# One step of a hybrid recurrent decoder: TensorE's order fixed by hand in the chain and the LRU stage, LRU begun among x's last projections, sample runs joined, products moved ahead of transpositions, projections reordered

## The chip, the core and the metric

The kernel runs on one core of one Trainium2 chip. The core's engines are TensorE (PE, matrix products; PEld is its weight load), VectorE (DVE), ScalarE (ACT), GpSimd (POOL) and SyncE (SP), which only issues transfers here. They run side by side and wait for one another by semaphores. The metric is the time of one execution in device microseconds (us). TensorE has a clock that is granted in steps; the profile gives it as a share of full speed.

## What is computed

One layer for 512 prompt tokens and 8 x 8 sample tokens (N = 576 columns), width 1024, all in float32. Cut to what matters:

```python
u, za, xb, zb, q, zc, gates = split_in(rmsnorm(x) @ w_in)
oa = rwkv7_branch(u, za, ...)      # per head: s = s*w + sa (kk*a) + v k,  o = s r
ob = rglru_branch(xb, zb, ...)     # conv, two gates, h = a*h + sqrt(1-a^2)*gate*xc
oc = cross_attn(q, zc, mem_k, mem_v)   # prompt: 256 memory rows; samples: own caches
g_a, g_b, g_c = split(sigmoid(gates), 3)
merged = g_a*(oa @ w_br_a) + g_b*(ob @ w_br_b) + g_c*(oc @ w_br_c)
y = rmsnorm(x + merged @ w_out)
```

## The kernel before

**Projections.** Every product with a weight matrix is cut into units of 128 output rows. A unit loads 512 KB of weights (`wraw`), ScalarE rounds them (`whi`, L280), VectorE subtracts (`wlo`, L281), and TensorE makes 48 products of 128\*128 with 288 columns: the high part with both halves of x, the low part with the high half (L355). Units wait in a list (`Stream`, L305 on); `st.go(n)` issues n steps of the unit in work, six products each, and `st.until(label)` issues until a unit is done. So the code of each stage says how many projections stand between its own small products. The weights of the next unit are fetched while the present one is in work. Units that a stage needs come first; the rest (`spill_units`: gates g, LRU input xb and gate zb, attention gate zc) fill in.

**What sets the order.** Each engine executes its instructions in one fixed order. A scheduler makes that order when the program is built, from the written order and its own costs. TensorE's too: a product written behind 37 units of projections can be put later or earlier than that.

**Stages.** Attention (L660 to L800) comes first: memory keys and values are projected (kv), the samples' caches come from DRAM in 512 KB tiles (`kn`), their keys are transposed (`skt`), scores sS and values sO are products of 32-column tiles. Then RWKV in four groups of two head pairs. For each group: `prep_a`, `prep_b`; `prep_c` (transpositions vt and bkt, then products m that give M, L990 to L996); `invert` (L1001): the diagonal blocks of M go to DRAM (d, L1006) and come back as X (L1011), VectorE solves 30 substitution steps in place (Xt and X, L1016 and L1018), copies the transpose XT, and xz and M's blocks return over DRAM (L1026 to L1032). Meanwhile `direct` makes R and Zt and `bonus` the bonus products, then 37 steps of projections. `invert2` needs xz: z (L1041) and w (L1050). `solved` makes U and W. Then the chain runs over eight chunks (`chain`, L1122 on): A from the state and ZR, UV plus A on VectorE, dS from UV and BKn, the state's sum, and the outputs (A again, L1113). Three runs for the samples (`sample_a`, `_b`, `_c`) stand behind chunks 1 to 6.

**LRU** (`lru_phase`): for eight blocks j a convolution, two gate products pg (L516), gates on ScalarE, a root over four blocks, and a scan (`scan`, L535 on): be = args \* gx on POOL (L543, L544), the scan he on VectorE (L546), its output times z, and a split into the operand oh, ol of branch b. All this runs beside the products of branches c and a (br2, br0); branch b (br1) needs the LRU's output. POOL adds branch a's products to `merged` (L452). Last comes the product with w_out (fo, L1349).

Of the kernel before, what the change touches and what calls it, by code (L numbers as in the profile page):

```python
# [9 lines left out]
F32 = mybir.dt.float32  # L10
# [8 lines left out]
P = 128  # L19
D = 1024  # L20
KC = 8
# [25 lines left out]
class Kern:  # L47
    def __init__(self, ctx, tc, ins, outs):
# [7 lines left out]
        self.dq = 0  # L56

# [4 lines left out]
    def transpose(self, out, in_, rows):  # L62

        self.nc.tensor.transpose(out, in_, self.ident[:rows, :rows])  # L64
# [151 lines left out]
    def softplus(self):  # L216
# [9 lines left out]
        nc.vector.tensor_scalar(self.c4, self.c4, -4.0, None, op0=ALU.mult)  # L226

# [77 lines left out]
class Stream:  # L305
# [24 lines left out]
    def step(self):  # L330
# [22 lines left out]
        for q, (a, b) in enumerate(((hi, xh), (hi, xl), (lo, xh))):  # L353
            for o, t0, m in parts:
                nc.tensor.matmul(self.ps[:, o:o + m], a[:, k, :], b[:, k, t0:t0 + m],  # L355
                                 start=(k == 0 and q == 0), stop=(k == KC - 1 and q == 2))
# [35 lines left out]
def spill_units(K, pool):  # L392
# [38 lines left out]
    us = [Unit(w, C_G + D * b + P * j, x, gate(K.gd[b, j]), f"g{b}{j}") for b in (2, 0, 1) for j in range(KC)]  # L431
    us += [Unit(w, C_ZC + P * j, x, silu2(K.ocz[j], K.ocd[j]), f"zc{j}") for j in range(KC)]
    us += [Unit(w, C_XB + P * j, x, conv_in(j), f"xb{j}") for j in range(KC)]
    us += [Unit(w, C_ZB + P * j, x, silu2(K.zbd[j]), f"zb{j}") for j in range(KC)]
    return us


def branch_units(K, pool, b, w, oh, ol, place, out=None):
# [3 lines left out]
    def mk(j):  # L442
        def use(pb):
# [7 lines left out]
            if place == "mid":  # L451
                nc.gpsimd.tensor_add(m, m, t)  # L452
# [7 lines left out]
def load_split(K, pool, src, oh, ol):  # L460
    nc = K.nc
    for k in range(KC):
# [5 lines left out]
def lru_phase(K, o2, then):  # L468
# [4 lines left out]
    with tc.tile_pool(name="lruc", bufs=1, reuse_waits="tile") as lc, tc.tile_pool(name="lru", bufs=2, reuse_waits="tile") as lp:  # L473
# [9 lines left out]
        ohl = []  # L483
# [21 lines left out]
        def gates(j):  # L505
            if j % 4 == 0:
                quad[j // 4] = lp.tile([P, 4, N], F32, tag="args", name="args")
# [3 lines left out]
            for q, bh in enumerate((K.bah, K.bxh)):  # L511
                g = lp.tile([P, N], F32, tag=f"g{q}", name=f"g{q}")
                for s in range(2):
                    pg = K.psb(f"pg{q}")[:, 0:HN]
                    cs = slice(HN * s, HN * s + HN)
                    nc.tensor.matmul(pg, wbd[q][:, j, :], xc[:, cs], start=True, stop=True)  # L516
# [3 lines left out]
            c4 = K.c4[:, j:j + 1]  # L520
            nc.vector.tensor_scalar(gr, gr, c4, c4, op0=ALU.mult, op1=ALU.add)
# [3 lines left out]
            nc.scalar.activation(ap_, gr[:, 0:TP], AF.Exp)  # L525
            nc.scalar.activation(as_[:, :, 1:9], smp(gr), AF.Exp)
            th = lp.tile([P, AE], F32, tag="th", name="th")[:, 0:N]
            nc.scalar.activation(th, gr, AF.Tanh, scale=-1.0)
            nc.scalar.activation(gr, gr, AF.Exp, scale=2.0)
            nc.vector.scalar_tensor_tensor(ar, gr, 1.0, th, op0=ALU.add, op1=ALU.mult)  # L530
            gx = lp.tile([P, N], F32, tag="gx", name="gx", bufs=4)
# [3 lines left out]
        def scan(j):  # L535
# [7 lines left out]
            nc.gpsimd.tensor_mul(bp_, ar[:, 0:TP], gx[:, 0:TP])  # L543
            nc.gpsimd.tensor_mul(bs_[:, :, 1:9], smp(ar), smp(gx))  # L544
# [5 lines left out]
            o = lp.tile([P, N], F32, tag="g0", name="lo")  # L550
            nc.vector.scalar_tensor_tensor(o[:, 0:TP], hp_, 0.5, z2[:, 0:TP], op0=ALU.mult, op1=ALU.mult)
            nc.vector.scalar_tensor_tensor(smp(o), hs_[:, :, 1:9], 0.5, smp(z2), op0=ALU.mult, op1=ALU.mult)
            split(nc, ohl[0][:, j, :], ohl[1][:, j, :], o)
# [4 lines left out]

        for j in range(4):
            conv(j)  # L560
            st.go(9 if j else 13)
            gates(j)
            if j == 3:
                then()
            st.go(3)
        st.until("br27")
        ohl = [o2.tile([P, KC, N], F32R, tag=tag, name=tag) for tag in ("oh", "ol")]
        roots(0)
        for j in range(4, KC):
            conv(j)  # L570
            st.go(4)
            scan(j - 4)
            st.go(3)
            gates(j)
            st.go(3)
        roots(4)
        for j in range(4, KC):
            scan(j)
            st.go(9)
# [7 lines left out]
    return ohl  # L587
# [72 lines left out]
def attention(K, xp, qs, qf, kv):  # L660


    nc, i, st = K.nc, K.i, K.st
# [3 lines left out]
    def p_scores(h, n):  # L667
# [3 lines left out]
        for tt in range(4):  # L671
            ps = K.psb(f"s{h}{tt}")
            for dc in range(2):
                for q, (a, b) in enumerate(((qh, kh), (qh, kl), (ql, kh))):
                    nc.tensor.matmul(ps[:, :NM], a[:, dc, tt * P:(tt + 1) * P], b[:, 2 * h + dc, :],
# [832 lines left out]
```

## Time and profile before

| | us |
|---|---|
| median of three runs | 1183.21 (1181.63 to 1183.48) |
| the profiled execution | 1184.47 |
| its span | 1182.7 |
| TensorE busy | 1145.4 (97%) |
| VectorE busy | 713.2 (60%) |
| ScalarE busy | 517.3 (44%) |
| POOL busy | 184.3 (16%) |
| attention, first kv product to first u product | 144.7 |
| first group, first U product to the end of its chain | 55.8 |
| last gate products of LRU to the product with w_out | 87.0 |

How to read it: the span is the profiled execution's first to last instruction; the profiled execution's time lies 1.26 us above the median. Busy shares are means over stages with different limits. A row of the timeline gives start, duration, engine, line, operation, the tile written and those read, the form (128\*64 is a product that uses 64 of the array's columns), the count, and in brackets the engine's idle time ahead with what ended it. A product of 288 columns is recorded once or twice, so a "x2" can be two products.

### The profile page before, as it was taken

Reading aid. Unit: us, or ns where it says so; the run is one execution under the profiler, and the core shown is the slowest. Engines: PE = TensorE matmul, PEld = TensorE weight load, DVE = VectorE, ACT = ScalarE, POOL = GpSimd, SP = SyncE. Lnnn points to the kernel's source line nnn. Section 1 sums busy time; section 2 is a strip of 40 time slices with the busy share of each in tenths; the row PEclk is TensorE's granted clock in tenths of the full one; section 3 lists DMA queues with packets and bytes.
Section 4 is the critical chain, followed back from the end, with each engine's and each line's share of the span. In section 5 each row is a group of like instructions: output and inputs, shape, how many; then the busy total and the mean of one; then the engine's idle time right before and its main releaser. Section 6 shows DMA issues by size and latency. Waiting matters only on the chain.

```text
span 1182.7 us, 25731 instructions
## 1 busy us (share of the span) xinstructions
PE 1145.4 (97%) x10567; PEld 1068.8 (90%) x10567; DVE 713.2 (60%) x1436; ACT 517.3 (44%) x1004; POOL 184.3 (16%) x311
## 2 busy tenths in 40 slices
PE   6999999999999999999999999999999999979997
PEld 4998877899998898988989989999889999979997
DVE  5345655238764687835788457874455386975633
ACT  5444544337324374243752336532444266442333
POOL 3010001010003210022100130101211012570031
PEclk9999999999999999999999999999999999998999
DMA  4447685522452233532233522345337665348412
GB/s 140 130 145 233 211 254 189 162 81 66 107 140 73 65 93 82 142 89 70 78 92 120 145 73 65 106 125 149 85 90 232 203 195 170 104 115 261 117 45 81
DMA packets 220623, 151.50 MB, mean 128 GB/s; under 512 B 52640, under 2 KB 196106, under 8 KB 220506
## 3 DMA queue, kind: packets, MB, share of 16 engines
q1 hardware_dynamic: 217242, 146.87, 42.1%
q10 hardware_dynamic: 3264, 2.99, 0.9%
q8 instruction: 83, 1.36, 0.5%
q14 instruction: 34, 0.28, 0.1%
HBM read 120.82 MB, written 29.01 MB: 127 GB/s over the span
## 4 chain that ended last, share of the span: by engine, by line
PE 79%; DVE 7%; ACT 5%; issue 3%; DMA 3%; POOL 2%; SPq 0%; DVEq 0%; ACTq 0%; POOLq 0%
PE u L355 13%; PE g L355 12%; PE br L355 9%; PE xb L355 4%; PE zc L355 4%; PE za L355 4%; PE fo L1349 4%; PE q L355 4%; PE zb L355 3%; PE kv L355 2%; PE m L990 1%; PE dS L1137 1%; DVE wlo L281 1%; DMA wraw<-in_w_mem_kv 1%; PE skt L64 1%
## 5 line engine op out<-in xcount | busy, mean ns | idle before, releaser
L280 ACT CAST whi<-wraw 128x1024 fp32r<-128x1024 f32 x129 | 135.4, 1050 | 292.6 <-PE g L355 90.7
L281 DVE TENSOR_TENSOR wlo<-wraw,whi 128x1024 fp32r<-128x1024 f32 x128 | 158.9, 1241 | 127.5 <-ACT whi L280 126.7
L355 PE MATMUL u<-xh,whi 128*128 128x288 f32 x400 | 92.2, 305 | 0.0
L355 PE MATMUL br<-oh,wlo 128*128 128x288 f32 x384 | 84.4, 302 | 4.4 <-DVE wlo L281 4.3
L355 PE MATMUL u<-xl,whi 128*128 128x288 f32 x400 | 88.6, 300 | 0.0
L355 PE MATMUL u<-xh,wlo 128*128 128x288 f32 x400 | 88.6, 299 | 0.0
L355 PE MATMUL br<-oh,whi 128*128 128x288 f32 x384 | 85.4, 305 | 3.0 <-ACT oh L592 2.9
L355 PE MATMUL g<-xh,whi 128*128 128x288 f32 x384 | 86.6, 304 | 0.0
L355 PE MATMUL g<-xh,wlo 128*128 128x288 f32 x384 | 84.7, 300 | 0.0
L355 PE MATMUL g<-xl,whi 128*128 128x288 f32 x384 | 84.4, 301 | 0.0
L355 PE MATMUL br<-ol,whi 128*128 128x288 f32 x384 | 84.2, 301 | 0.0
L355 PEld LDWEIGHTS u<-xh,whi 128*128 128x128 f32 x400 | 65.1, 188 | 5.5 <-issue 4.1
L355 PEld LDWEIGHTS br<-oh,wlo 128*128 128x128 f32 x384 | 63.5, 194 | 5.6 <-DVE wlo L281 5.6
L355 PEld LDWEIGHTS br<-oh,whi 128*128 128x128 f32 x384 | 63.7, 193 | 4.3 <-ACT oh L592 3.4
L355 PEld LDWEIGHTS u<-xl,whi 128*128 128x128 f32 x400 | 64.7, 188 | 2.0 <-issue 1.4
L355 PEld LDWEIGHTS u<-xh,wlo 128*128 128x128 f32 x400 | 64.7, 188 | 0.9 <-issue 0.2
L355 PEld LDWEIGHTS g<-xh,whi 128*128 128x128 f32 x384 | 62.3, 190 | 3.2 <-issue 3.1
L355 PEld LDWEIGHTS g<-xh,wlo 128*128 128x128 f32 x384 | 62.7, 190 | 1.2 <-issue 1.2
L355 PEld LDWEIGHTS br<-ol,whi 128*128 128x128 f32 x384 | 63.4, 193 | 0.1
L355 PEld LDWEIGHTS g<-xl,whi 128*128 128x128 f32 x384 | 62.4, 190 | 1.1 <-issue 1.1
L1016 DVE TENSOR_TENSOR Xt<-X 72x30 f32<-72x30 f32 (+14 forms) x120 | 39.3, 328 | 11.4 <-DMA X<-d 7.8
L1349 PE MATMUL fo<-wol,oh 128*128 128x256 f32 (+1 forms) x160 | 45.0, 282 | 0.0
(386 smaller groups left out, 2894.3 us busy)
## 6 DMA issues: line engine op xcount, KB each, us to landing
wraw<-in_w_in SPq DMA_DIRECT2D x89, 512.0 KB
wraw<-in_w_mem_kv SPq DMA_DIRECT2D x16, 512.0 KB
kn<-in_cache_mem_k SPq DMA_DIRECT2D x16, 512.0 KB
kn<-in_cache_mem_v SPq DMA_DIRECT2D x16, 512.0 KB
gd<-flt SPq DMA_DIRECT2D x24, 288.0 KB
gtt<-gd SPq DMA_DIRECT2D x24, 288.0 KB
wraw<-in_w_br_c SPq DMA_DIRECT2D x8, 512.0 KB
wraw<-in_w_br_a SPq DMA_DIRECT2D x8, 512.0 KB
```

The source lines that it names most:

```text
L64: self.nc.tensor.transpose(out, in_, self.ident[:rows, :rows])
L280: nc.scalar.copy(hi, raw)
L281: eng.tensor_sub(lo, raw, hi.bitcast(F32))
L355: nc.tensor.matmul(self.ps[:, o:o + m], a[:, k, :], b[:, k, t0:t0 + m], start=(k == 0 and q == 0), stop=(k == KC - 1 and q == 2))
L990: nc.tensor.matmul(pms[h][64 * w:64 * w + 64, P * (c - c0):P * (c - c0) + P], BK[64 * h:64 * h + 64, c, w, :], ZR[64 * h:64 * h + 64, c].r ...
L1016: nc.vector.tensor_mul(tv, X[:, 0:s, s:s + 1].to_broadcast([NQ, s, m]), X[:, s:s + 1, s + 1:].to_broadcast([NQ, s, m]))
L1137: nc.tensor.matmul(pS[hs, C * o.q:C * o.q + C], o.BKn[:, c, hs], o.UV[:, c, hs], start=True, stop=True, tile_position=(0, 64 * h))
L1349: nc.tensor.matmul(pos[t][:r, :W], a[:, k, t * P:t * P + r], b[:, k, :], start=(k == 0 and q == 0), stop=(k == KC - 1 and q == 2))
```

## The change

It does these things:

- `K.mm` and `K.transpose` pin a product into the written order while `K.pin` is set. It is set from `invert2` to the end of each group's chain, and in all of `lru_phase`. There the order on TensorE, projections included, is as written.
- `products` (m and M) comes ahead of `prep_c`'s transpositions, and the writes of d follow each pair's M; X's read is issued ahead of the transpositions. The filler ahead of `invert2` is 34 steps instead of 37, and `invert2` does both halves of z before both of w.
- The chain's filler is given per step (2 and 4 steps; 1 and 3 in the last group), and the sample runs stand next to chain products of the same form (`full`, `tiled`).
- Attention: keys are transposed from the q stage on, and sample scores and values stand in longer runs; loads of values are issued ahead.
- x's projections: zb, sixteen of g, xb, four of g, zc, four of g (before: g, zc, xb, zb).
- LRU begins after zc7 with four units of g left; branch units are added when x's are done. be and the sum into `merged` move from POOL to VectorE; the factor c4 goes into ScalarE's scale and bias. The splits of the LRU's first four outputs stand behind br27 (branch c's end), and the writes of the LRU's state rows behind br11.

```diff
+        if self.pin:
+            self.tc.keep_in_program_order(ins)
...
-    us = [... g ...]; us += [zc]; us += [xb]; us += [zb]
+    return zb + g[:16] + xb + g[16:-4] + zc + g[-4:]
...
-                nc.gpsimd.tensor_add(m, m, t)
+                nc.vector.tensor_add(m, m, t)
...
-            nc.gpsimd.tensor_mul(bp_, ar[:, 0:TP], gx[:, 0:TP])
-            nc.gpsimd.tensor_mul(bs_[:, :, 1:9], smp(ar), smp(gx))
+            nc.vector.tensor_mul(bp_, ar[:, 0:TP], gx[:, 0:TP])
+            nc.vector.tensor_mul(bs_[:, :, 1:9], smp(ar), smp(gx))
...
             for o in prs:
                 prep_b(o)
                 st.go(3)
+                scaled(o)
+                products(o)
+                st.go(3)
+            X = invert()
             for o in prs:
                 prep_c(o)
-                st.go(6)
-            invert(prs)
+                st.go(3)
+            substitute(prs, X)
             direct(prs)
             for o in prs:
                 bonus(o)
-            st.go(37)
+            st.go(34)
+            K.pin = True
             invert2(prs)
             solved(prs)
...
+            fulls = {1: lambda: sample_a(o0), 4: lambda: sample_c(o0), 5: lambda: sample_a(o1)}
+            tileds = {2: lambda: sample_b(o0), 3: lambda: [sample_o(o0), sample_in(o1)],
+                      6: lambda: sample_b(o1), 7: lambda: sample_o(o1)}
             for c in range(8):
-                chain(prs, c)
-                if c in (1, 4): ... sample_a, sample_b, sample_c
+                chain(prs, c, (2, 4) if g + 1 < NG else (1, 3), fulls.get(c, none), tileds.get(c, none))
+            K.pin = False
...
+        K.pin = True
+        conv(0)
+        st.go(8)
+        conv(1)
+        st.go(6)
+        gates(0)
+        ...
+        for j in (4, 5, 6):
+            conv(j + 1)
+            st.go(4)
+            then(range(3 * j - 12, min(3 * j - 9, KC)))
+            st.go(3)
+            gates(j)
+        st.until("br27")
+        ohl = operand(o2)
+        ...
+        gates(7)
+        roots(4)
         for j in range(4, KC):
+            st.go(5)
             scan(j)
-            st.go(9)
+            split(nc, ohl[0][:, j, :], ohl[1][:, j, :], keep[j][1])
+        K.pin = False
```

**z on TensorE, second group.** Before (g and u are projections, z the first product behind the inversion, of one pair at a time; 300 projections stand between the last m product and this z):

```order
L355 MATMUL g_6133<-xl,whi 128x288 x2
L355 MATMUL g_6133<-xh,wlo 128x288 x2
L355 MATMUL u_6210<-xh,whi 128x288 x2
L1041 MATMUL z_5925<-xz,M_5235 32x32 x9
L355 MATMUL u_6210<-xl,whi 128x288 x2
L355 MATMUL u_6210<-xh,wlo 128x288 x2
L355 MATMUL u_6210<-xh,whi 128x288 x2
L355 MATMUL u_6210<-xl,whi 128x288 x2
L355 MATMUL u_6210<-xh,wlo 128x288 x2
```

Now (every product of `K.mm` has that helper's line, L71; the two pairs take turns from the first z on, 214 projections behind the last m):

```order
L71 MATMUL g_6061<-xh,whi 128x288 x2
L71 MATMUL g_6061<-xl,whi 128x288 x2
L71 MATMUL g_6061<-xh,wlo 128x288 x2
L71 MATMUL z_6092<-xz,M_5348 32x32
L71 MATMUL z_6093<-xz,M_5492 32x32
L71 MATMUL z_6092<-xz,M_5348 32x32
L71 MATMUL z_6093<-xz,M_5492 32x32
L71 MATMUL z_6092<-xz,M_5348 32x32
L71 MATMUL z_6093<-xz,M_5492 32x32
```

z of both pairs moved to one place, with nothing between the first pair's z and the second's.

**A chain step on TensorE, first group, with the samples' transposition s0t.** Before:

```order
L1128 MATMUL A<-sbd_2475,ZR 128x128 x2
L355 MATMUL u_4497<-xl,whi 128x288 x2
L355 MATMUL u_4497<-xh,wlo 128x288 x2
L1137 MATMUL dS<-UV,BKn 64x64 x2
L355 MATMUL u_4598<-xh,whi 128x288
L1137 MATMUL dS<-UV,BKn 64x64 x2
L1113 MATMUL A<-UV,M_3281 64x64
L1113 MATMUL A<-UV,M_3428 64x64
L1113 MATMUL A<-UV,M_3281 64x64
L1113 MATMUL A<-UV,M_3428 64x64
L355 MATMUL u_4598<-xh,whi 128x288
```

Now:

```order
L65 MATMUL s0t<-ident,sn 128x128 x4
L71 MATMUL g_4369<-xh,whi 128x288 x2
L71 MATMUL g_4369<-xl,whi 128x288 x2
L71 MATMUL g_4369<-xh,wlo 128x288 x2
L71 MATMUL g_4369<-xh,whi 128x288 x2
L71 MATMUL g_4369<-xl,whi 128x288 x2
L71 MATMUL g_4369<-xh,wlo 128x288 x2
L71 MATMUL dS<-UV,BKn 64x64 x4
L71 MATMUL A<-UV,M_3393 64x64
L71 MATMUL A<-UV,M_3538 64x64
L71 MATMUL A<-UV,M_3393 64x64
L71 MATMUL A<-UV,M_3538 64x64
```

dS of both pairs stands in one piece and A behind it; the projections that stood inside moved ahead of dS and behind A. Counted over the whole program, neighbouring products change between whole-array and tiled form 332 times before and 210 times now.

**A scan of LRU on VectorE.** Before (he is the scan, gtt a branch's gate product, wlo the next unit's weights):

```order
L530 SCALAR_TENSOR_TENSOR args<-g_12440,th 128x576
L281 TENSOR_TENSOR wlo<-wraw,whi 128x1024
L546 SCALAR_TENSOR_TENSOR he<-ae,be 128x584 x2
L551 SCALAR_TENSOR_TENSOR lo<-he,z_12488 128x512
L552 SCALAR_TENSOR_TENSOR lo<-he,z_12488 128x64
L450 SCALAR_TENSOR_TENSOR gtt<-gtt,br_12503 128x576
L281 TENSOR_TENSOR wlo<-wraw,whi 128x1024
L593 TENSOR_TENSOR ol<-lo,oh 128x576
L551 SCALAR_TENSOR_TENSOR lo<-he,z_12575 128x512
L552 SCALAR_TENSOR_TENSOR lo<-he,z_12575 128x64
```

Now (be and the sum into merged stand here too):

```order
L294 TENSOR_TENSOR wlo<-wraw,whi 128x1024
L466 TENSOR_TENSOR merged<-merged,gtt 128x576
L557 TENSOR_TENSOR be<-args,gx 128x512
L558 TENSOR_TENSOR be<-args,gx 128x8x8
L557 TENSOR_TENSOR be<-args,gx 128x512
L560 SCALAR_TENSOR_TENSOR he<-ae,be 128x584
L558 TENSOR_TENSOR be<-args,gx 128x8x8
L564 SCALAR_TENSOR_TENSOR gx<-he,z_12318 128x512
L565 SCALAR_TENSOR_TENSOR gx<-he,z_12318 128x64
L560 SCALAR_TENSOR_TENSOR he<-ae,be 128x584
L464 SCALAR_TENSOR_TENSOR gtt<-gtt,br_12305 128x576
```

The product be, which POOL made, moved in front of the scan on VectorE, and the sum into merged in front of that. On TensorE 312 projections stand between the last gate products and branch b's first product, before 162.

More of the change, by code (lines that the diff above doesn't have):

```diff
@@ L62, in transpose, with mm @@
     def transpose(self, out, in_, rows):
-        self.nc.tensor.transpose(out, in_, self.ident[:rows, :rows])
+        ins = self.nc.tensor.transpose(out, in_, self.ident[:rows, :rows])
+        if self.pin:
+            self.tc.keep_in_program_order(ins)
+    def mm(self, *a, **kw):
+        ins = self.nc.tensor.matmul(*a, **kw)
+        if self.pin:
+            self.tc.keep_in_program_order(ins)
+        return ins
     def psb(self, name):
@@ L226, in softplus @@
         nc.vector.tensor_scalar(self.c4, self.c4, -4.0, None, op0=ALU.mult)
+        self.c4n, self.c8 = (self.cst.tile([P, 8], F32, name=n) for n in ("c4n", "c8"))
+        nc.vector.tensor_scalar(self.c4n, self.c4, -1.0, None, op0=ALU.mult)
+        nc.vector.tensor_scalar(self.c8, self.c4, 2.0, None, op0=ALU.mult)
     def norm_load(self, tp, src, rows):
@@ L465, in load_split, with lru_phase @@
         split(nc, oh[:, k, :], ol[:, k, :], t)
-def lru_phase(K, o2, then):
+def lru_phase(K, o2, merge, operand):
     nc, tc, i, pv = K.nc, K.tc, K.i, K.pv
@@ L557, in roots, with lru_out @@
             nc.scalar.activation(q4, q4, AF.Sqrt, scale=0.25)
-        for j in range(4):
[L560 to L570, printed above, removed]
+        K.pin = True
[4 more added lines that the diff above has]
+        gates(0)
+        conv(2)
+        st.go(5)
+        gates(1)
+        st.until("g17")
+        oa, then = merge()
+        conv(3)
+        st.go(4)
+        gates(2)
+        st.go(5)
+        gates(3)
+        st.go(5)
+        roots(0)
+        for j in range(4):
+            scan(j)
+            if j == 1:
+                conv(4)
+            st.go(5)
+        for j in (4, 5, 6):
+            conv(j + 1)
             st.go(4)
-            scan(j - 4)
+            then(range(3 * j - 12, min(3 * j - 9, KC)))
             st.go(3)
             gates(j)
+        st.until("br27")
+        ohl = operand(o2)
+        for j in range(4):
+            split(nc, ohl[0][:, j, :], ohl[1][:, j, :], keep[j][1])
             st.go(3)
+        gates(7)
         roots(4)
         for j in range(4, KC):
+            st.go(5)
             scan(j)
-            st.go(9)
+            split(nc, ohl[0][:, j, :], ohl[1][:, j, :], keep[j][1])
+        K.pin = False
+    return ohl, lambda: lru_out(K, lo_st, cv_st)
+def lru_out(K, lo_st, cv_st):
     lf = lo_st.rearrange("p a b -> p (a b)")
@@ L1035, in invert2, with half @@
         def invert2(prs):
-            for g0 in (0, 9):
+            def half(g0):
                 pzs = [K.psb("z1") for o in prs]
@@ L1054, in invert2 @@
                     nc.scalar.copy(o.M1[a:a + 32, g0:g0 + 9, b:b + 32], pw[a:a + 32, 0:288].rearrange("p (a b) -> p a b", b=32))
+            half(0)
+            half(9)
+            st.go(1)
+            above(0)
+            above(9)
+            st.go(3)
         def direct(prs):
@@ L1121, in plus_state, with chain @@
                 nc.vector.tensor_add(u, pA[o.br:o.br + 64, P * o.q:P * o.q + P], u)
-        def chain(os, c):
+        def chain(os, c, steps, full, tiled):
             cur, nxt = sbd[(c + 1) % 2], sbd[c % 2]
@@ L1148, in chain @@
                 o.cur = nxt[:, o.q, :]
-            st.go(4)
+            tiled()
+            st.go(steps[1])
         def state_out(o):
```

339 lines of the change are left out of this document (184 added, 155 removed).

## Prediction

> **What bounds the kernel now.** I read the page's totals first, then the chain of work that ended last, then single stretches of TensorE's timeline. The totals and the chain's shares:
>
> ```profile
> PE 1145.4 (97%) x10567; PEld 1068.8 (90%) x10567; DVE 713.2 (60%) x1436; ACT 517.3 (44%) x1004; POOL 184.3 (16%) x311
> PE 79%; DVE 7%; ACT 5%; issue 3%; DMA 3%; POOL 2%; SPq 0%; DVEq 0%; ACTq 0%; POOLq 0%
> ```
>
> TensorE is the bound, and the change neither adds nor removes a matmul (8807 in each program). So it can pay in two ways only: the same matmuls issue more densely, or TensorE waits less. Two prices come first. A stretch of the chain gives the pace of projections; a timeline of TensorE in the first group's chain gives the price of changing between whole-array matmuls (128\*128) and tiled ones:
>
> ```profile
> 466.62 36.80 PE g L355 x276
> ...
> 378.93 0.45 PE L1137 MATMUL dS<-UV,BKn 128*64 128x64 f32 x8
> 379.21 0.41 PE L1113 MATMUL A<-UV,M 128*64 128x64 f32 x8
> 379.55 0.53 PE L355 MATMUL u<-xh,whi 128*128 128x288 f32 x2
> ...
> 386.32 0.60 PE L64 MATMUL s0t<-ident,sn 128*128 128x128 f32 x4
> 386.75 0.61 PE L1128 MATMUL A<-sbd,ZR 128*128 128x128 f32 x4
> ...
> 387.82 0.34 PE L1137 MATMUL dS<-UV,BKn 128*64 128x64 f32 x4
> 388.09 0.40 PE L355 MATMUL u<-xh,whi 128*128 128x288 f32 x1
> 388.42 0.34 PE L1137 MATMUL dS<-UV,BKn 128*64 128x64 f32 x4
> 388.58 0.40 PE L1113 MATMUL A<-UV,M 128*64 128x64 f32 x8
> 388.92 0.40 PE L355 MATMUL u<-xh,whi 128*128 128x288 f32 x1
> ```
>
> A projection costs 36.80/276 = 0.133 us, a transposition (386.75 − 386.32)/4 = 0.11. One projection between two dS pairs takes 388.42 − 388.09 = 0.33 instead of 0.13, so each of its two changes costs 0.10. Compared whole, the step with that projection inside takes 388.92 − 387.82 = 1.10, less 0.13 for the projection 0.97; the step with both pairs together takes 379.55 − 378.93 = 0.62. That is 0.35 for two changes, 0.17 each, because the tiled matmuls also overlap better when more stand together.
>
> **Part 1, the order on TensorE.** Counted in the two orders, 332 changes of tile form become 210: 98 fewer in the four groups (inversion and chain), 24 fewer in attention. 122 at 0.10 is 12 us, at 0.17 it is 21. I take 19.5 (0.16 each), as most removed ones are of the dS kind. The Trainium skill ("TensorEngine Tiling (Array Packing)", Tiling Modes, Key Properties) says that a change of tiling mode drains TensorE and a change of tile alone does not. By that rule alone the gain would be the isolated 0.10 and this term 12; the 0.35 for two agrees with the drain but goes beyond it.
>
> **Part 2, z now has a fixed place.** z, the first product after the 32x32 inversions, needs a round trip: M from the last m product, d to DRAM, X back, VectorE's substitution, XT, d, xz back. TensorE, the SP queue and VectorE in the second group, and VectorE's groups of instructions from 468 to 498 us:
>
> ```profile
> 457.64 0.43 PE L990 MATMUL m<-ZR,BK 64*64 64x128 f32 x4
> 461.13 2.31 PE L1065 MATMUL R<-UV,M 64*64 64x64 f32 x72
> 503.61 0.75 PE L1041 MATMUL z<-xz,M 32*32 32x32 f32 x18
> ...
> 461.56 1.04 SPq L1006 DMA_DIRECT2D d<-M  x2
> 466.10 0.31 SPq L1011 DMA_DIRECT2D X<-d  x1
> ...
> 469.33 0.19 DVE L1016 TENSOR_TENSOR Xt<-X 72x30 f32<-72x30 f32 x1 [1.59 <-DMA X<-d]
> 495.79 0.21 DVE L1018 TENSOR_TENSOR X<-X,Xt 72x30 f32<-72x30 f32 x1
> ...
> 500.88 0.50 SPq L1029 DMA_DIRECT2D xz<-d  x1
> ...
> L1016 DVE TENSOR_TENSOR Xt<-X 72x30 f32<-72x30 f32 (+14 forms) x30 | 9.8, 328 | 2.5 <-DMA X<-d 1.6
> L1018 DVE TENSOR_TENSOR X<-X,Xt 72x30 f32<-72x30 f32 (+14 forms) x30 | 9.8, 327 | 0.9
> L281 DVE TENSOR_TENSOR wlo<-wraw,whi 128x1024 fp32r<-128x1024 f32 x5 | 6.1, 1219 | 1.3 <-ACT whi L280 1.3
> ```
>
> From the last m (457.64) to the second xz's issue (500.88) are 43.2 us. Its landing is not shown; X, four times as large, took 469.33 − 466.10 = 3.2, so z's data are there at about 46.5 after the last m. Before, z waited for nothing: 300 projections stood ahead of it, and no wait for xz is in the table of waits. Now z and all behind it keep the written order, and 214 projections (200 in the first group) stand between the last m and z. Cover: 214 × 0.133 = 28.5; 36 transpositions that moved behind the products, 3.9; R, Zt and bonus 466.62 − 461.13 = 5.5; changes and m itself 0.8: 38.7 us. The path gets shorter by about 1 us, since no other transfer stands between the writes of d and X on SP's queue any more, and by nothing else: four weight splits (wlo, 1.2 us each) still stand inside the substitution, and three of the bonus products move into it. So z waits 46.5 − 38.7 − 1 = 6.8 us, 1.9 longer in the first group and less in the last, which has three wlo inside. I take 4 × 6.8 = 27 us lost. Ends: 2 each (the wlo leave the substitution, 4.9 us) and 10 each (bonus and wlo late).
>
> **Part 3, the clock behind a wait.** What a wait of TensorE does to the clock shows where sample values arrived late in attention, in the timeline and in the same stretch by windows (the figure behind POOL's is the granted clock):
>
> ```profile
> 213.63 0.64 PE L752 MATMUL sO<-kn,pts 128*32 128x256 f32 x8 [2.01 <-DMA kn<-in_cache_mem_v]
> 215.06 0.68 PE L355 MATMUL g<-xh,wlo 128*128 128x288 f32 x2
> 215.53 0.68 PE L355 MATMUL g<-xh,whi 128*128 128x288 f32 x2
> ...
> 213.80:217.20 3.40, 3.40 (x21) 3.00 (x14) 0.00 (x0) 1.14 (x2) 0.00 (x0) 0.61 0.58 203
> ```
>
> After a wait of 2.01 us projections start every (215.53 − 215.06)/2 = 0.24 us for 3.4 us: 14 of them, 0.107 lost on each, 1.5 us. Twice that, 3.0, if the slow stretch lasts double. I take 1.75 for each z, 7 us; ends 0 and 12. The Trainium skill ("TensorE: Matmul & The Clock Gate", Part 1, What's actually happening) gives half rate after an idle window of about 3.4 us. By that rule a z wait of 2 us would cost no clock; by the row it costs 1.5, and the row decides. For 6.8 us both give half rate.
>
> **Part 4, the LRU stage.** The last stretch of branch products, the attention stretch, and the waits:
>
> ```profile
> 1031.80:1118.80 87.00, 79.51 (x553) 77.67 (x552) 56.59 (x64) 30.63 (x41) 26.96 (x28) 0.94 0.53 161
> 78.50:223.20 144.70, 140.91 (x1131) 117.06 (x1130) 74.82 (x150) 63.15 (x122) 8.94 (x21) 0.99 0.68 211
> ...
> PE br L355 <- DVE wlo L281: 4.3, 4, 3.0
> PE br L355 <- ACT oh L592: 2.9, 1, 2.9
> PE m L990 <- DVE M L996: 2.3, 4, 0.6
> PE sO L752 <- DMA kn<-in_cache_mem_v: 2.0, 1, 2.0
> PE dS L1137 <- DVE UV L1121: 1.2, 5, 0.3
> ...
> 1044.90 1.30 POOL L543 TENSOR_TENSOR be<-args,gx 128x512 f32<-128x512 f32 x1 [1.92 <-ACT args L557]
> 1046.51 2.44 DVE L546 TENSOR_TENSOR_SCAN he<-ae,be 128x584 f32<-128x584 f32 x1 [3.59 <-POOL be L544]
> 1050.39 0.67 DVE L551 SCALAR_TENSOR_TENSOR lo<-he,z 128x512 f32<-128x512 f32 x1
> ```
>
> TensorE lost 87.00 − 79.51 = 7.5 us idle and about (1 − 0.94) × 87 = 5.2 to the clock there: 12.7. VectorE stood 3.59 us in a scan that waited for POOL's product, and the weight split (wlo) that TensorE needed was queued behind it. Now VectorE makes that product itself (about 0.67, as the like-sized row at 1050.39), and 312 projections instead of 162 stand between the last gates and the last branch's first product, 41.6 us instead of 21.6. VectorE's extra load, 8 × (0.67 + 0.22) and 8 sums of 0.74, is 13 us in a stage where it has 87.00 − 56.59 = 30 us free; the wlo of branch a then stand behind up to 8 us of LRU work, against 6.4 us per weight tile (48 projections), caught up within two tiles. I take 11 of the 12.7; ends 4 and 12.7. The gates' tables (c4, c4n, c8) only take work from VectorE; 0.
>
> **Part 5, small things.** The waits of m for M and of dS for UV (2.3 + 1.2) go, as more projections stand there now (12 in a chain step, 6 in the last group), and some of the shorter ones behind them: 4 us, ends 0 and 6. In attention the sample keys' transpositions move ahead; 211 GB/s over the stretch leaves the kn wait as it is, or makes up to 8 us of new ones: I take 0. LRU begins among x's last projections, where the first gates stand 84 projections (11.2 us) after zc7, behind the splits of branch c's operand on VectorE: 0 to 5 us, I take 0. The new order of x's projections swaps cover of equal kind: 0, hidden under the prefetch of one weight tile.
>
> **Sum**, against the profiled execution's 1184.47: −19.5 − 11 − 4 + 27 + 7 = −0.5, so 1184.0. That execution lay 1.26 above the median of 1183.21; against the median, about 1182.7, and I say 1182.
>
> **Rivals.**
> - z's data come in time. For it: the transfers of d and X are the first thing on SP after M, and VectorE is emptier while TensorE stands. Against it: 19.6 us of pure substitution and four DRAM transfers stay. With 2 us each and no loss of clock: 1183.2 − 34.5 + 8 = 1157.
> - z decides the other way. If it waits over 34.5/4 = 8.6 us per group, clock included, the kernel is slower; at 10 us and two slow stretches (13 each) it is 1183.2 − 34.5 + 52 = 1201. For it: the first group's shorter cover, and the bonus products that now stand between the first steps of the substitution. Against it: the 1 us saved on SP.
> - The LRU stall stays, because VectorE now carries more: then 11 less gain, 1193, with the like-sized wait for wlo in the table.
> - Attention becomes bound by its transfers: 8 us, 1190.
>
> **Chances.** About even, as summed (1172 to 1192): 0.43, of which 0.18 lies below 1180.8, 0.13 within 0.2% of the median and 0.12 above. z in time: 0.27 (1148 to 1171). z longer, or the LRU stall or attention's transfers on top: 0.30 (1193 to 1210). A measurement of this kernel can tell about 0.2%, 2.4 us, from nothing. Faster 0.27 + 0.18 = 0.45, same 0.13, slower 0.12 + 0.30 = 0.42. The range 1152 to 1204 leaves out the ends of the outer cases; the likeliest alone has 1172 to 1192.
>
> **What would show it.** Right: in the changed kernel's table of waits, z (or PE at its line) stands for xz's transfer four times with 5 to 9 us, each followed by projections at 0.24 us; dS pairs and A run in one piece; no wait of br for wlo above 1 us. Wrong: no wait of z at all (then the substitution ran faster or the count of cover is off), or a wait of sO or skt for kn that is longer than 3 us, or of pg for xc at the start of LRU.

## The result, and the profile after

| | us |
|---|---|
| before, median of four runs | 1183.35 (1181.63 to 1184.37) |
| after, median of four runs | 1204.27 (1202.81 to 1206.39) |
| ratio after to before | 1.0184, 95% interval 1.0171 to 1.0197 |
| the profiled execution after | 1204.39, span 1202.4 |

The change makes the kernel 1.8% slower, 20.9 us between the medians. The forecast was 1182 with a range up to 1204; what came true is the rival in which z's data come so late that z decides. Two executions of later runs that took much longer than the others of the same kernel (1221.45 without the pin, 2712.90 with the four steps given back) are left out of the medians below.

The totals of the changed kernel, the shares of the chain of work that ended last, and TensorE's waits (what waits, on what, us in total, times, longest):

```profile
PE 1128.5 (94%) x10567; PEld 1066.5 (89%) x10567; DVE 707.8 (59%) x1454; ACT 522.4 (43%) x1004; POOL 152.7 (13%) x287
PE 70%; DVE 14%; DMA 8%; ACT 4%; issue 3%; SPq 1%; ACTq 0%; DVEq 0%
...
PE z L71 <- DMA xz<-d: 37.4, 8, 8.7
...
PE m L71 <- DVE M L1047: 5.7, 7, 1.2
...
PE br L71 <- DVE wlo L294: 1.4, 1, 1.4
```

TensorE is busy 17 us less for the same matmuls (1128.5 instead of 1145.4), and the span still grew by 19.7. The chain moved from TensorE (79% to 70%) to VectorE and the transfers (together 10% to 22%): that is the round trip of z, which was under projections before. z waits 37.4 us in all: 9.4, 11.1, 9.8 and 7.1 in the four groups. Before, it waited for nothing.

TensorE around z, second group. Brackets give its idle time:

```profile
480.40 0.43 PE L71 MATMUL m<-ZR,BK 64*64 64x128 f32 x4
...
527.94 0.31 PE L71 MATMUL z<-xz,M 32*32 32x32 f32 x2 [8.65 <-DMA xz<-d]
530.65 2.13 PE L71 MATMUL z<-xz,M 32*32 32x32 f32 x70 [2.40 <-DMA xz<-d]
532.71 0.85 PE L71 MATMUL g<-xh,whi 128*128 128x288 f32 x2
533.36 0.68 PE L71 MATMUL g<-xl,whi 128*128 128x288 f32 x2
533.84 0.68 PE L71 MATMUL g<-xh,wlo 128*128 128x288 f32 x2
534.45 2.13 PE L71 MATMUL w<-M,xz 32*32 32x32 f32 x72
```

The first pair's z waits 8.65 us, the second pair's 2.40 more. Behind that, projections start every 0.24 us ((533.84 − 533.36)/2), the half pace of the prediction's row in attention.

**Where the 19.7 us are.** I divided both traces at the same products, and set aside the projections that moved from one stretch to another at 0.133 us each. Two stretches of the changed kernel in windows, the first group's chain (U to the state's end) and LRU's last stretch (granted clock in the column behind POOL's):

```profile
372.30:436.50 64.20, 64.04 (x726) 60.19 (x726) 35.71 (x78) 25.79 (x55) 15.79 (x26) 1.00 0.31 80
...
1044.70:1138.70 94.00, 94.00 (x703) 93.57 (x702) 58.96 (x77) 32.62 (x40) 8.28 (x11) 1.00 0.57 169
```

The chain of the first group took 55.8 with 245 projections and takes 64.2 with 336: 12.1 for the 91, so the chain itself got 3.7 cheaper. In LRU's last stretch TensorE is busy all 94.00 us at full clock; before it lost 12.7 there.

| stretch | span after − before | projections moved in | at 0.133 | left |
|---|---|---|---|---|
| start and attention | +12.3 | +144 | +19.2 | −6.9 |
| four times R to U (z and w inside) | −15.0 | −459 | −61.2 | +46.2 |
| four chains, U to the state's end | +27.9 | +332 | +44.3 | −16.4 |
| between the groups, ahead of the first and behind the last (m products inside) | −21.5 | −230 | −30.7 | +9.2 |
| LRU, first gates to the product with w_out | +16.6 | +213 | +28.4 | −11.8 |
| end | −0.3 | | | −0.3 |

The column adds up to 20.0; the 0.3 beside 19.7 comes from rounding and from where the stretches end. So the gains of the forecast are there (chains, attention and LRU: −35.1), and z with what hangs on it takes more than they give.

### The profile page after: what moved, and what is told of

It reads as the page before. It is cut to its first block, busy times and chain, and to the rows that moved or that the text cites. A ratio compares the mean times of both kernels' runs of the same rounds, so it can differ in the third digit from the quotient of the medians.

```text
span 1202.4 us, 25686 instructions
## 1 busy us (share of the span) xinstructions
PE 1128.5 (94%) x10567; PEld 1066.5 (89%) x10567; DVE 707.8 (59%) x1454; ACT 522.4 (43%) x1004; POOL 152.7 (13%) x287
## 4 chain that ended last, share of the span: by engine, by line
PE 70%; DVE 14%; DMA 8%; ACT 4%; issue 3%; SPq 1%; ACTq 0%; DVEq 0%
PE u L71 14%; PE br L71 11%; PE g L71 7%; PE za L71 4%; PE fo L71 4%; PE q L71 4%; DVE wlo L294 3%; DVE X L1087 3%; DVE Xt L1085 3%; PE zc L71 2%; PE A L71 2%; PE zb L71 2%; PE xb L71 2%; PE kv L71 2%; DMA wraw<-in_w_mem_kv 1%
## 5 line engine op out<-in xcount | busy, mean ns | idle before, releaser
L71 PE MATMUL u<-xh,whi 128*128 128x288 f32 x400 | 89.5, 305 | 0.0
L71 PE MATMUL g<-xh,whi 128*128 128x288 f32 x384 | 88.9, 312 | 0.0
L71 PE MATMUL g<-xh,wlo 128*128 128x288 f32 x384 | 87.4, 307 | 1.1 <-DVE wlo L294 1.1
L71 PE MATMUL g<-xl,whi 128*128 128x288 f32 x384 | 86.4, 306 | 0.0
L71 PE MATMUL u<-xl,whi 128*128 128x288 f32 x400 | 85.9, 296 | 0.0
L71 PE MATMUL u<-xh,wlo 128*128 128x288 f32 x400 | 85.8, 296 | 0.0
L71 PE MATMUL br<-oh,wlo 128*128 128x288 f32 x384 | 82.5, 297 | 1.4 <-DVE wlo L294 1.4
L71 PE MATMUL br<-oh,whi 128*128 128x288 f32 x384 | 83.5, 299 | 0.0
L71 PE MATMUL br<-ol,whi 128*128 128x288 f32 x384 | 82.2, 296 | 0.0
L71 PEld LDWEIGHTS u<-xh,whi 128*128 128x128 f32 x400 | 63.7, 189 | 6.5 <-issue 6.1
L71 PEld LDWEIGHTS g<-xh,wlo 128*128 128x128 f32 x384 | 64.8, 196 | 1.9 <-DVE wlo L294 1.3
L71 PEld LDWEIGHTS g<-xh,whi 128*128 128x128 f32 x384 | 64.7, 197 | 1.8 <-issue 1.0
L71 PEld LDWEIGHTS g<-xl,whi 128*128 128x128 f32 x384 | 64.6, 196 | 1.0 <-issue 1.0
L71 PEld LDWEIGHTS u<-xh,wlo 128*128 128x128 f32 x400 | 64.6, 188 | 0.0
L71 PEld LDWEIGHTS u<-xl,whi 128*128 128x128 f32 x400 | 64.5, 188 | 0.0
L71 PEld LDWEIGHTS br<-oh,wlo 128*128 128x128 f32 x384 | 61.8, 188 | 1.9 <-DVE wlo L294 1.9
L71 PEld LDWEIGHTS br<-oh,whi 128*128 128x128 f32 x384 | 62.2, 189 | 0.6
L71 PEld LDWEIGHTS br<-ol,whi 128*128 128x128 f32 x384 | 61.8, 188 | 0.0
L1199 DVE TENSOR_TENSOR UV<-A,UV 64x128 f32<-64x128 f32 x64 | 18.5, 289 | 56.6 <-PE A L71 55.5
L1265 POOL TENSOR_TENSOR zx<-ZR,bm 128x256 f32<-128x256 f32 x16 | 16.7, 1052 | 224.5 <-DVE X L1087 103.8
```

Source lines behind the costliest of these rows:

```text
L71: ins = self.nc.tensor.matmul(*a, **kw)
L1199: nc.vector.tensor_add(u, pA[o.br:o.br + 64, P * o.q:P * o.q + P], u)
L1265: nc.gpsimd.tensor_mul(zx[:, w], o.ZR[:, 8, w, :].rearrange("p (g t) -> p g t", g=2).unsqueeze(2).to_broadcast([P, 2, 4, 32]), K.bm4.unsqu ...
```

## Experiments

**More cover ahead of z.** Theory: z is late because too few projections stand ahead of it. The next group's projections are made available earlier, 14 more steps stand ahead of z in the first three groups (a step is six products, 0.8 us), and the chain gets fewer.

```diff
             st.go(34)
-            K.pin = True
-            invert2(prs)
-            solved(prs)
             if g + 1 < NG:
                 lora_w(g + 1)
                 st.add(*group_units(g + 1))
+                st.go(14)
+            K.pin = True
+            invert2(prs)
+            solved(prs)
...
-                chain(prs, c, (2, 4) if g + 1 < NG else (1, 3), ...)
+                chain(prs, c, (1, 3), ...)
```

> The changed kernel, with z's place filled: in the first three groups 84 more projections (298 instead of 214; 284 in the first) stand between the last m and z, taken from the chain's filler (1 and 3 steps instead of 2 and 4). All else is as changed. Theory 'z's place': the path from the last m to z's data is fixed (46 to 50 us), and TensorE's stream is the same but for its order, so the z waits of the first three groups (9.4, 11.1 and 9.8 us) go to 0 to 1 us and the slow clock behind them (about 2.8 us each) with them: 1204 - 30 - 8 + 1 = about 1167 us; the last group still waits about 7 us. Rival 'pinning as such' (a fixed order makes TensorE late in many places, z is only where it shows): the time stays above 1190, with new waits of dS for UV or of A for sbd in the chain, whose filler is now shorter.

Measured 1175.53 (1171.84 to 1180.92), ratio to before 0.994 (0.9915 to 0.9964): 28.7 faster than the changed kernel. Its waits:

```profile
PE dS L71 <- DVE UV L1199: 9.0, 12, 1.0
PE z L71 <- DMA xz<-d: 7.1, 2, 6.4
```

z waits in the last group alone, which kept its cover. That lack of cover cost the time is shown. The second group from R to U, in the kernel before, the changed one and this one, with 319, 221 and 305 projections:

```profile
461.10:514.20 53.10, 53.10 (x578) 51.82 (x577) 30.34 (x75) 15.74 (x28) 2.70 (x4) 1.00 0.51 140
...
487.50:540.60 53.10, 42.03 (x480) 40.82 (x479) 27.81 (x75) 13.33 (x26) 1.87 (x3) 0.84 0.34 93
...
479.60:528.60 49.00, 48.98 (x562) 48.19 (x561) 30.34 (x77) 16.29 (x29) 1.98 (x3) 1.00 0.42 117
```

With the 84 moved projections set aside, this stretch is 14.2, 15.2 and 13.8 us shorter in the first three groups than in the changed kernel. The time is still 8 above the expected 1167, since the rival came true in part: dS now waits 9.0 for UV, as the one step left in the chain is too short for VectorE's sum, and the three chains together lose 17.6.

**Bonus early.** Theory: bonus stands at the head of VectorE's queue, waits there for TensorE, and holds back the substitution behind it. It is moved ahead of `prep_c`'s transpositions.

```diff
             X = invert()
+            for o in prs:
+                bonus(o)
...
             direct(prs)
-            for o in prs:
-                bonus(o)
```

> The changed kernel, with the bonus products written ahead of prep_c's transpositions, so that VectorE's bonus multiplications do not stand in front of the substitution's first step. Cover ahead of z is unchanged (214 projections, 195 in the first group). Theory 'the path is VectorE's queue': X had landed some 4 us before the first step, which stood behind bonus multiplications waiting for TensorE; now it starts about 2 to 4 us earlier and has three multiplications of 0.45 us fewer inside, so each z wait shrinks by 3.5 to 5.5 us, 14 to 22 us in all: 1182 to 1190 us. Rival 'the transfers set it' (X, d and xz over DRAM): the first step does not start earlier, z's waits stay at 37 us in sum, 1202 to 1205 us.

Measured 1190.78 (1185.39 to 1191.13), ratio to before 1.0056 (1.0037 to 1.0076): 13.5 faster than the changed kernel. Its wait of z, and in the second group the last m, X's read, the first and the last substitution step, and the second xz's issue:

```profile
PE z L71 <- DMA xz<-d: 23.7, 8, 7.6
...
473.81 0.44 PE L71 MATMUL m<-ZR,BK 64*64 64x128 f32 x4
...
479.99 0.36 SPq L1076 DMA_DIRECT2D X<-d  x1
...
484.86 0.19 DVE L1085 TENSOR_TENSOR Xt<-X 72x30 f32<-72x30 f32 x1 [0.56 <-DMA X<-d]
...
510.14 0.21 DVE L1087 TENSOR_TENSOR X<-X,Xt 72x30 f32<-72x30 f32 x1
...
515.52 0.49 SPq L1098 DMA_DIRECT2D xz<-d  x1
```

z waits 13.7 less in all, but not evenly: 0.9, 5.8, 4.7 and 2.3 in the four groups. In the second group the first step now waits for X, not behind bonus, and starts 11.05 behind the last m, where the changed kernel needs 12.2. That is only 1.2. From there to the last step's end are 25.5 us instead of 28.45 (3.0 less: the bonus products are gone from the substitution, and a split of small weights waits 0.34 for ScalarE there instead of 1.25), and from there to the second xz's issue 5.2 instead of 6.66 (1.5 less).

**No pin.** The changed order as written, with the scheduler free to shift products:

```diff
-        K.pin = True      # lru_phase
+        K.pin = False
...
-            K.pin = True  # ahead of invert2
+            K.pin = False
```

> The changed kernel with nothing pinned: the scheduler orders all of TensorE again, LRU included; the written order is as changed. It puts 271 to 282 projections between the last m and z and makes 252 changes of tile form instead of 210. Theory: z's waits fall from 37 to about 6 us and their slow clock from 11 to about 4, while the 42 extra changes cost 0.17 us each, 7 us: 1204 - 31 - 7 + 7 = about 1173 us. Rival 'the order pays more than the waits cost' (fixed order is worth more than 0.17 us a change, LRU's above all): above 1185 us, with waits of br for wlo back in the LRU stage.

Measured 1165.27 (1163.54 to 1168.49, three executions), ratio to before 0.9854 (0.9832 to 0.9875): 39.0 faster than the changed kernel, by two lines. Of the waits:

```profile
PE z L71 <- DMA xz<-d: 3.3, 2, 2.3
PE dS L71 <- DVE UV L1199: 3.1, 3, 1.4
```

The scheduler puts 271 to 282 projections ahead of z instead of 214; 252 changes of form stand in its order instead of 210. So the fixed place, with the cover that it has here, is what costs, and the rest of the change (order written in runs, LRU) is worth about 17 us even without it.

**LRU's products back on POOL**, in the changed kernel:

```diff
-                nc.vector.tensor_add(m, m, t)
+                nc.gpsimd.tensor_add(m, m, t)
...
-            nc.vector.tensor_mul(bp_, ar[:, 0:TP], gx[:, 0:TP])
-            nc.vector.tensor_mul(bs_[:, :, 1:9], smp(ar), smp(gx))
+            nc.gpsimd.tensor_mul(bp_, ar[:, 0:TP], gx[:, 0:TP])
+            nc.gpsimd.tensor_mul(bs_[:, :, 1:9], smp(ar), smp(gx))
```

> The changed kernel with be and the sum into merged on POOL again, as before the change; order and cover in the LRU stage are otherwise the changed ones. Theory 'cover': the 312 projections between the last gates and branch b's first product (before 162) alone took the LRU stall away: the stage stays at 94 us, total 1204 to 1206. Rival 'VectorE's wait for POOL': scans wait for POOL's product again and the weight splits queue behind them, so a part of the old 12 us comes back, with waits of br for wlo of 3 us and more: 1208 to 1216.

Measured 1215.11 (1212.88 to 1216.64), ratio to before 1.0268 (1.025 to 1.0285): 10.8 slower than the changed kernel. TensorE's waits for the weight split, then a scan behind POOL, the split queued behind it and TensorE's wait for that split, and LRU's last stretch:

```profile
PE br L71 <- DVE wlo L294: 7.7, 2, 4.0
...
1059.76 2.45 DVE L560 TENSOR_TENSOR_SCAN he<-ae,be 128x584 f32<-128x584 f32 x1 [3.48 <-POOL be L558]
...
1069.31 2.41 DVE L294 TENSOR_TENSOR wlo<-wraw,whi 128x1024 fp32r<-128x1024 f32 x1
...
1071.78 0.53 PE L71 MATMUL br<-oh,wlo 128*128 128x288 f32 x2 [3.77 <-DVE wlo L294]
...
1049.90:1150.00 100.10, 95.60 (x703) 95.03 (x702) 56.73 (x62) 32.17 (x40) 27.61 (x26) 0.98 0.54 161
```

The chain of the prediction's part 4 is back: POOL's be late, VectorE standing in the scan, the weight split behind it, TensorE without weights. The stretch takes 100.10 instead of 94.00, and the one ahead of it, which holds the other wait, 96.90 instead of 91.70. So cover alone, the theory of this run, did not take the stall away.

**The same move alone, in the kernel before** (the edit above the other way round):

> The kernel before, with only be and the sum into merged moved from POOL to VectorE. Theory 'the scan's wait for POOL' (the changed kernel with these on POOL took 11 us more): the stall of the last LRU stretch goes, the stage falls from 87 to about 76 us, total 1171 to 1174 us. Rival 'cover and move are both needed' (with 162 projections the scans still push the weight splits too late): a part of the stall stays, 1176 to 1182 us.

Measured 1179.33 (1177.94 to 1181.83), ratio to before 0.9967 (0.9955 to 0.998): 4 faster than the kernel before, not 11. LRU's last stretch there, and TensorE's waits:

```profile
1030.10:1112.20 82.10, 76.87 (x552) 75.83 (x551) 53.80 (x73) 28.27 (x37) 6.02 (x15) 0.96 0.56 170
...
PE br L355 <- DVE wlo L281: 2.5, 2, 2.1
PE ro L64 <- POOL lru_st L549: 2.3, 1, 2.3
```

TensorE still stands 5.2 of 82.10 us, with 162 projections ahead of branch b. With 312 and VectorE both, it stands 0.0 of 94.00: the gain needs both halves.

**Both xz reads first** on SP's queue, ahead of the reads of M's blocks:

```diff
             nc.sync.dma_start(d1, XT)
-            nc.sync.dma_start(d2, X)
             for o in prs:
                 ... xz of o <- d1
+            nc.sync.dma_start(d2, X)
+            for o in prs:
                 ... M's blocks of o <- d2
```

> The changed kernel, with both pairs' xz read back one behind the other, ahead of the reads of M's blocks (before, two reads of M stood between them on SP's queue). Theory 'SP's order is a part of the path': the second xz is issued about 1.4 us earlier, and z's second waits (0.8, 2.4, 1.7 and 0.6 us, 5.6 in sum) shrink to about 0.4 each; M's blocks arrive later but w has some us of room: 1199 to 1202 us. Rival 'the landing, not the issue, sets it' (both transfers share the engines): z's second waits stay, 1203 to 1206 us.

Measured 1199.61 (1195.27 to 1201.89), ratio to before 1.0137 (1.011 to 1.0164): 4.7 faster than the changed kernel. TensorE at z in the second group:

```profile
528.54 0.31 PE L71 MATMUL z<-xz,M 32*32 32x32 f32 x2 [8.56 <-DMA xz<-d]
529.07 2.12 PE L71 MATMUL z<-xz,M 32*32 32x32 f32 x70 [0.21 <-DMA xz<-d]
```

The first pair waits as long as in the changed kernel, the second 0.21 instead of 2.40. Over the four groups z waits 32.9 instead of 37.4, so the order of reads on SP is worth about 1 us per group.

**A dS pair split.** One filler step moved between the two pairs' dS, in the changed kernel, which raises the changes of form from 210 to 274:

```diff
             for o in os:
+                if o is not os[0]:
+                    st.go(1)
                 ... dS of o
...
-            st.go(steps[1])
+            st.go(steps[1] - 1)
```

> The changed kernel (1204.3 us), with one step of projections (6 products) moved from behind each chain step to between the two pairs' dS, in all 32 chain steps: the same products, 64 more changes of tile form (274 instead of 210); z and all waits of the groups stay. Theory (0.17 us per change, as the whole step with a projection inside showed): + 11 us, 1213 to 1217 us. Rival (0.10, the price of one isolated change): + 6 us, 1209 to 1212.

Measured 1220.78 (1209.34 to 1222.73), ratio to before 1.0296 (1.0248 to 1.0344). The first chain in windows:

```profile
370.50:437.50 67.00, 66.56 (x725) 60.89 (x725) 35.28 (x78) 25.87 (x55) 15.19 (x26) 1.00 0.28 74
```

67.00 instead of 64.20: 2.8 us for 16 changes, 0.175 each; the other three chains are 2.7, 2.9 and 3.2 longer. That is the price the prediction read from two single steps as 0.17, not the 0.10 of one isolated change. The total does not show it as plainly. 64 changes make 11.2 us, so 1215. The profiled execution, 1209.34 at a granted clock of 0.972, lies lower: a stretch at half clock between the first and the second group (part 5 below) is missing in it (3.0), and the start and the stretches from R to U are 3.2 shorter. The median, at a clock of 0.962, lies 5 higher; where those executions lost it no timeline shows, and that stays open.

**All of it, with the pin.** Bonus early, xz first, ten more steps ahead of z (four in the last group), and (2, 2) steps in the chain instead of (2, 4):

```diff
+            st.go(10 if g + 1 < NG else 4)
             K.pin = True
             invert2(prs)
             solved(prs)
...
-                chain(prs, c, (2, 4) if g + 1 < NG else (1, 3), ...)
+                chain(prs, c, (2, 2) if g + 1 < NG else (1, 3), ...)
```

> The changed kernel with its order still pinned, and four things together: 10 steps (60 projections) moved from the chain's second filler to ahead of z in the first three groups, 4 steps in the last; the chain's filler 2 and 2 steps, so that dS keeps its 12 projections behind A; bonus ahead of the transpositions; both xz read first. Theory: cover is 44 to 47 us (42 in the last group) against a path of 43 to 45 (41), so z waits under 1 us each; no slow clock in the groups; dS does not wait as it did with 6 projections. Changed kernel's time less z's waits and clock (49 us) less the 1 to 2 us of what R to U overlaps: 1150 to 1158 us. Rival 'the short second filler makes A wait for sbd': 12 projections (1.6 us) hide a sum of 0.6 us and a queue on VectorE of up to 1.2; if they do not, 0.5 us in 21 steps, 10 us, 1160 to 1168.

Measured 1158.06 (1156.42 to 1160.37), ratio to before 0.9792 (0.9769 to 0.9816). Waits, the second group's z and U, and its stretch from R to U:

```profile
PE pg L71 <- issue: 6.7, 1, 6.7
...
PE dS L71 <- DVE UV L1200: 2.4, 2, 1.2
...
PE z L71 <- DMA xz<-d: 1.3, 3, 0.9
...
509.01 1.33 PE L71 MATMUL z<-xz,M 32*32 32x32 f32 x72
...
515.12 1.09 PE L71 MATMUL U<-r,M 64*64 64x64 f32 x30
...
472.00:515.10 43.10, 43.10 (x518) 42.30 (x517) 27.38 (x70) 15.59 (x28) 3.59 (x3) 1.00 0.41 114
```

The time is at the upper end of what was expected. z hardly waits, and TensorE is busy through the stretch at full clock. The new wait, 6.7 at LRU's first gates (pg), is the four steps that the last group took: they are missing there.

**The same without the pin** (no steps added, since the scheduler finds the cover):

> The changed kernel with nothing pinned (1166.9 us) and with bonus ahead of the transpositions and both xz read first. The scheduler puts 258 to 266 projections between the last m and z (cover 45 us). Theory: the path is 3.5 to 5 us shorter, so z waits for nothing, and the remaining waits of z (3.3) and of dS for UV (3.1) shrink: 1160 to 1165 us. The difference to the pinned kernel of the same edits is then the price of the 32 more changes of tile form, 32 x 0.17 = 5 us, and what it waits more. Rival: no gain (1165 to 1169), because the scheduler shortens the cover with the path.

Measured 1162.55 (1159.15 to 1164.79), ratio to before 0.9825 (0.9801 to 0.9849). z isn't among the longer waits. Pinned it is 4.5 us faster than this, although that run still has the wait of pg. The 32 more changes of form that its expectation counts are 3 to 6 us at 0.10 to 0.175, so with enough cover the fixed order seems to pay by them. The two runs also spread their filler differently, and no run has the pin as its only difference from this one, so the 4.5 is not shown to be the price of the order alone.

**The last group's four steps given back to LRU**:

```diff
-            st.go(10 if g + 1 < NG else 4)
+            st.go(10 if g + 1 < NG else 0)
```

> The kernel of e7 (1158.1 us), without the 4 steps that its last group took from the units kept for LRU's start: there TensorE's queue stood 6.7 us ahead of the first gates and ran at half clock behind it. Theory 'the filler is one sum, and taking it from LRU only moved the wait': the wait ahead of pg (6.7 us) goes; the last group's z has 38.8 us of cover against a path of about 41 and waits about 2 us, with about 2 us of slow clock: 1150 to 1156 us. Rival: the wait ahead of the gates has another cause (the change of pools) and stays; z's wait comes on top, 1159 to 1163.

Measured 1157.57 (1151.12 to 1158.10, four executions), ratio to before 0.9764 (0.9735 to 0.9794), a little above the expected 1150 to 1156. The same kernel ran again, for a profile that shows its waits:

> The kernel of e9 once more, whose profile could not be read. Its median (1157.9 us) is that of e7 (1158.1), so one of two things holds. Theory: the wait ahead of the first gates (6.7 us in e7) is gone, and the last group's z waits instead, with slow clock, 5 to 7 us in sum: the filler is one sum. Rival: the wait ahead of the gates is still there (another cause), and z's wait in the last group is below 1 us, so that nothing changed.

Measured 1156.25 (two executions, 1156.06 and 1156.44), ratio to before 0.9769 (0.9727 to 0.9811). Its waits:

```profile
PE m L71 <- DVE M L1047: 5.7, 7, 1.2
...
PE z L71 <- DMA xz<-d: 4.8, 3, 3.8
```

The wait of pg is gone and z waits again in the last group: projections are one sum, and what one place gets another lacks. With the half clock behind the wait, that group's stretch from R to U loses 8.5 us, more than the expected 5 to 7 (43.6 with 209 projections, where the third group takes 43.1 with 269). This kernel and the one with four steps in the last group are the fastest: 1156 to 1158, 2% under the kernel before and 4% under the changed one.

## Why the prediction was wrong

**Part 1, order on TensorE: mechanism right, size too small.** Forecast −19.5 at 0.16 per change; measured 0.175 in the split-dS run. Chains and attention together give −23.3, of which 1.8 is the wait of sO for kn, forecast to stay (2.0 before, 0.2 after). R to U gains another 2.2 per group, which z's wait hides: in the run with more cover the second group takes 49.0 us with 305 projections, before 53.1 with 319, and 14 projections are 1.9. Taking the last group like the other three, that is 8.8 more, so −32.1.

**Part 4, LRU: right.** Forecast −11, measured −11.8 in the balance and 10.8 in the run with POOL. That the move alone gives only 4 shows that the second half of the argument, 312 projections of cover, was needed for it. The wait of br for wlo was said to be gone above 1 us; one of 1.4 is left.

**Part 2, z: the failed step.** The mechanism was right, the length of the path not: z waits 37.4 us instead of 27, so 9.4 instead of 6.8 per group. The cover was right: from the last m (480.40) to the end of the projections ahead of z (527.94 − 8.65 = 519.29) are 38.9 us in the second group, forecast 38.7. The path was forecast 45.5 long and took 50.25 (480.40 to the second z at 530.65). VectorE and SP of the changed kernel in the second group, behind the last m at 480.40:

```profile
483.40 0.39 SPq L61 DMA_DIRECT2D wraw<-in_w_in  x1
485.07 0.31 SPq L1076 DMA_DIRECT2D X<-d  x1
...
492.26 0.46 DVE L1020 TENSOR_TENSOR bon<-bon,v 128x288 f32<-128x288 f32 x1 [3.70 <-PE bon L71]
492.64 0.18 DVE L1085 TENSOR_TENSOR Xt<-X 72x30 f32<-72x30 f32 x1
...
500.58 0.42 DVE L628 TENSOR_TENSOR wls<-wl,wls 128x256 fp32r<-128x256 f32 x1 [1.25 <-ACT wls L627]
...
520.89 0.20 DVE L1087 TENSOR_TENSOR X<-X,Xt 72x30 f32<-72x30 f32 x1
...
525.91 0.32 SPq L1098 DMA_DIRECT2D xz<-d  x1
526.85 0.85 SPq L1101 DMA_DIRECT2D M<-d  x2
527.75 0.50 SPq L1098 DMA_DIRECT2D xz<-d  x1
```

- SP helped more than the 1 us that I allowed: X's read is issued 4.7 behind the last m, before 8.5, though a weight read still stands between it and the writes of d, where I had said that no other transfer would. At the 3.2 us of the earlier row X was there at about +7.9.
- It brought nothing, because VectorE stood from there on. bonus is the instruction ahead of the first step in its queue and waited 3.70 us for TensorE's bonus product, which stands behind R and Zt. The first step starts at +12.2; I had forecast 10.7, so 1.5 too late. I had read that bonus products would stand among the steps, but the path's sum has no term for them, neither for their own time nor for what the first of them waits for. In the third and fourth groups the first step is as late; in the first it comes at +7.7, and bonus's wait, 4.26 us there, stands right behind it.
- From the first step to the last are 28.45 us (492.64 to 521.09), before 26.67 (469.33 to 496.00): three bonus products now stand inside, and a split of the small weights that waits 1.25 us for ScalarE. 1.8, which I had as "nothing else".
- From the last step to the second xz's issue are 6.66, before 4.88. The first xz is issued 0.8 later behind the last step than before, and two reads of M's blocks stand between the two xz where one stood, 0.9. 1.8, which I had not looked at.

1.5 + 1.8 + 1.8, less 0.3 for xz's landing, is the 4.8 by which the path was longer than said. Both orders, on VectorE and on SP, could be read before the run.

**Part 3, clock: mechanism right, size not.** I took 1.75 per z, from a stretch of 3.4 us at half pace. The half pace lasts longer (the slow part of the first group, in windows):

```profile
355.50:372.60 17.10, 11.12 (x174) 10.30 (x176) 0.25 (x1) 3.83 (x9) 0.84 (x1) 0.50 0.32 68
```

The 17.10 us include 6 of the wait; the rest is z, w and the projections behind them. In the second group, from z's first product to U with the second pair's wait left out, are 10.2 us (527.94 to 540.55, less 2.40); in the pinned run with cover the same products take 6.1 at full clock (509.01 to 515.12). That is 4.1 for this group, and by the same comparison 4.7, 3.9 and 4.7 for the others: 17.4 instead of 7. The run with more cover says the same: R to U of the first three groups is 43.2 shorter there, 30.3 of it the wait, which leaves 12.9 for the clock, 4.3 each; with 4.7 for the last group that is 17.6. (The balance has only 46.2 for the stretch, since it also holds the 8.8 that the order gains in it.)

**Part 5: wrong in sign.** The waits of dS for UV are gone, as forecast. The waits of m were to go too; they are 5.7 now, 2.3 before. The wait is of m for M, inside `products`, where no projection stands between a pair's products any more. One is followed by a slow stretch:

```profile
462.83 0.44 PE L71 MATMUL m<-ZR,BK 64*64 64x128 f32 x4 [1.16 <-DVE M L1047]
...
464.70:471.50 6.80, 6.80 (x39) 6.51 (x39) 4.80 (x13) 2.45 (x3) 1.43 (x1) 0.50 0.17 52
```

This stretch between the first and the second group takes 51.1 us, the two like it 48.1 with the same 227 projections: 3.0 for the slow clock. The same wait of 1.16 stands in all three, so it does not bring the slow stretch each time; in the split-dS run it brought none. With the 3.4 of longer waits that is 6.4 of the +9.2; the other 2.8 I have not traced. Every variant of the changed kernel whose waits can be read has the 5.7, so no run tells what would lift it.

**The sum again.** From the forecast's −0.5: order 12.6 better (−32.1, not −19.5), z's wait 10.4 worse (37.4, not 27), its clock 10.6 worse (17.6, not 7), between the groups 13.2 worse (+9.2, not −4), LRU 0.8 better, end 0.3 better: +20.0. So three terms of about the same size went wrong, z's wait, its clock and the stretches with the waits of m, which I had listed as a gain; the order paid for one of them.

**The rivals.** That z decides was set at a wait over 8.6 per group, clock included, and 1201 for 10 us and two slow stretches: measured 9.4 with 4.4 of clock, and 1204. That the total comes so near to 1201 is partly luck, since the waits of m and the larger gain of the order, which this rival did not have, nearly cancel. Its point for, bonus products between the first steps, was the right one. The point against it, time saved on SP, was true and did not count, as VectorE was the later of the two.

## What to carry to other kernels

When a consumer is given a fixed place by hand, add up what stands ahead of it and set it against its producer's whole path, with every instruction that is queued ahead on the other engines priced by what it waits for and not by its own duration: a scheduler may have been filling that gap unseen (300 projections before, 214 after). Projections used as filler are one sum, so cover for z comes out of the chain or out of LRU, and the path is better shortened first (bonus early 13.5, xz first 4.7). Once the cover is there, a fixed order that keeps like forms together seems to pay: the pinned run was 4.5 us faster here, with the filler spread differently too.

## What the runs showed of the hardware

- A change between whole-array and tiled matmuls cost 0.175 us in its place (2.8 us for 16), nearly twice the 0.10 of the single one that the prediction's row shows.
- Waits of 7 to 11 us left TensorE at a granted clock of 0.50 for 13.7 to 17.1 us, beginning inside the wait, where the 2.01 us wait in the kernel before was followed by 3.4. What followed z is many small tiled products, and in the second group full pace (a projection every 0.135 us) came back only at 539.9, 12 us after z began.
- One wait of 1.16 us (m), among small products, was followed by 6.80 us at 0.50; two more of the same length in the same execution were not.
